# Four grouped weight tiles: high parts feature by feature, low parts last and on VectorE

## The chip, the cores and the metric

One core of one Trainium2 chip runs the whole program. The metric is device time in microseconds for one execution, the median of several runs of the same program.

## What is computed

The program takes 512 tokens of width 1024 through a gMLP layer and a FoX attention layer, each followed by a SwiGLU feed-forward network (FFN), and then through a block of mLSTM and indexer-selected attention with a gated embedding at its end. All inputs, weights and results are float32. What matters here are three products of a normalised and modulated activation with a weight matrix:

```python
def swiglu(h, w_gu, w_down):          # FFN 0 and FFN 1: w_gu is 1024 x 5632
    gu = h @ w_gu
    g, u = jnp.split(gu, 2, axis=-1)
    return (jax.nn.silu(g) * u) @ w_down
...
    u = rmsnorm(h, norm_in[i])        # second block
    proj = u @ w_in[i]                # its first columns here: the indexer's
```

## The kernel before

**Three passes per product.** Every large product is exact to more than one float32r pass: each operand is split into a high part `hi` (rounded to float32r) and a low part `lo` (the rest), and `mm3` (line 415) sums three passes of TensorE, weights' high by activations' high (line 416), high by low (line 417), and weights' low by activations' high (line 418). In a feature-major product the weights are the stationary operand.

**Preparing a weight tile.** `wsplit` (line 274) loads 128x1024 weights to a buffer `raw` (four buffers, loads issued on SP's queue, line 271), copies them to `whi` on ScalarE (line 279) and subtracts to get `wlo` (line 282). `share` decides which engine subtracts: with `share=n` every n-th low part, counted by a program-wide counter `lo_n`, goes to GpSimd, the others to VectorE. There are four buffers each of `whi` and `wlo`.

**Feature-major products.** `gemm_a` (line 420) gives out^T, a tile of 128 outputs by 512 tokens at a time, with 8 feature tiles k of 128 to sum over. Its first `group` tiles are taken together and by halves of the tokens, since the second 256 tokens of the activation come later:

```python
for c in halves:
    for (wh, wl), pt in zip(ws, accs):
        for k in range(KD):
            mm3(pt[0:m, c], wh[...k...], wl[...k...], hi[k][:, c], lo[k][:, c], ...)
```

So a group of four tiles is 2 halves x 4 tiles x 8 features x 3 passes = 192 passes of 256 columns, tile by tile. Three calls have a group: the FFN's at line 586 (twice, with `GG = (1, 1)`) and the indexer's at line 1226 (`IG = 1`). With these constants all four low parts of each group are made on GpSimd.

**What comes before a group.** In all three places the preceding product is a token-major `gemm_b` (line 443) whose last chunks go token tile by token tile (128 tokens each). As a token tile is through, `post` (line 534) evacuates its PSUM accumulator `acc` (a square on ScalarE, line 541, and a multiply on VectorE, line 542), adds it to the residual (line 552) and normalises the row (`norm_rows`, lines 366, 367, 359, 360, 370). After each second token tile, `to_T` (line 372) transposes two tiles on TensorE (line 384), scales them on ScalarE (line 407, or 405 in the second block) and splits them on VectorE: `hi` by a cast (line 408) and `lo` by a subtraction (line 409). So half the tokens of the group's activation come while `gemm_b` still works on the other half.

**PSUM.** The pool `ps` has four accumulators `acc` and four banks `tp`. The four token tiles of `gemm_b` hold the four accumulators; a group of four weight tiles takes the same four, each after its evacuation.

**Order.** Every engine works through its own instructions in a fixed order. Apart from one section of layer 0, that order is not the written one: the compiler places an instruction that is ready by its own estimate ahead of earlier-written ones that are not, and prefers the earlier-written where several are ready.

Of the kernel before, what the change touches and what calls it, by code (L numbers as in the profile page):

```python
"""One-core Trainium2 kernel: a gMLP layer, a FoX attention layer (each with a SwiGLU FFN), then an
mLSTM + indexer-sparse-attention block with a per-layer-embedding gate, for 512 tokens of width 1024.

Large products run as three float32r passes over exactly split operands (hi*hi + hi*lo + lo*hi).
"""
# [55 lines left out]
# ------------------------------------------------------------------ host layout  # L61
def _wa(w):
    """[K, N] -> [N/128, 128 (k in tile), K/128 * 128]: stationary chunks of 128 outputs."""
    k, n = w.shape
    return np.ascontiguousarray(
        w.reshape(k // P, P, n // P, P).transpose(2, 1, 0, 3).reshape(n // P, P, (k // P) * P))


def _wb(w):
    """[K, N] -> [N/512, K/256, 128, 2 * 512]: moving chunks of two k tiles by 512 outputs."""  # L70
    k, n = w.shape
    return np.ascontiguousarray(
        w.reshape(k // 256, 2, P, n // 512, 512).transpose(3, 0, 2, 1, 4).reshape(n // 512, k // 256, P, 1024))
# [26 lines left out]
def layout(i):  # L100
# [33 lines left out]
    # gMLP  # L134
# [14 lines left out]
    # FoX  # L149
# [8 lines left out]
    # second block  # L158
# [3 lines left out]
    # rows of the last tile: keys 0-63, input gates 64-67, forget gates 96-99, indexer weights 100-107  # L162
# [28 lines left out]
# ------------------------------------------------------------------ kernel body  # L191
def body(tc, nc, a):
    V, S_, G, PE = nc.vector, nc.scalar, nc.gpsimd, nc.tensor

    with ExitStack() as es:
# [55 lines left out]
        # ---------------- constants  # L251
# [14 lines left out]
        # ---------------- weights: load, split  # L266
# [7 lines left out]
        def wsplit(src, n=1024, share=0, alloc=None, raw=None):  # L274
            """share: every share-th low part on GpSimd"""
# [9 lines left out]
        # ---------------- modulation vectors, worked off between weight chunks  # L285
# [21 lines left out]
        def fill(n=1):  # L307
            """one column's load, and the product for the one loaded before"""
# [25 lines left out]
        def gain(csc, gname):  # L334
            """gain * (1 + scale), a column per feature tile"""
# [5 lines left out]
        def gb_row(cg, gname):  # L341
            """gate * gain, on every partition"""
# [13 lines left out]
        # ---------------- norms, transposes  # L356
        def rsq(out, ss, scale):
            """out = 1 / sqrt(ss * scale + eps)"""
# [3 lines left out]
        def norm_rows(xr, out):  # L362
            """out = xr / rms(xr), a token tile in two halves"""
# [8 lines left out]
        def to_T(ts, xn, g, sh, hi, lo, js=range(KD), spill=None):  # L372
            """token-major halves of the tiles ts -> feature-major hi, lo; what is transposed goes
            to spill as well"""
# [39 lines left out]
        # ---------------- products  # L414
# [5 lines left out]
        def gemm_a(h, w, n, evac, m=P, group=0, nfill=0, share=0, gshare=1):  # L420
            """out^T tile i (m outputs by 512 tokens), weights stationary. The first group goes by
            halves of the tokens, since the second half of h comes later."""
            hi, lo = h
            i = 0
            while i < n:
                run = list(range(i, min(n, i + (group if i == 0 and group else 1))))
                halves = (slice(0, 256), slice(256, 512)) if i == 0 and group else (slice(0, 512),)
                ws, accs = [], []
                for q in run:
                    ws.append(wsplit(w[q], KD * m, gshare if len(run) > 1 else share))  # L430
                    accs.append(acc())
                    if len(run) == 1:
                        fill(nfill if i >= 10 or not group else 0)
                for c in halves:
                    for (wh, wl), pt in zip(ws, accs):
                        for k in range(KD):
                            mm3(pt[0:m, c], wh[:, k * m:(k + 1) * m], wl[:, k * m:(k + 1) * m],
                                hi[k][:, c], lo[k][:, c], k == 0, k == KD - 1)
# [4 lines left out]
        def gemm_b(h, w, groups, kt, evac, head=False, tail=0, nfill=0, share=0, raws=(), hshare=1):  # L443
            """out tile (g, t): 128 tokens by 512 outputs, activations stationary. The last chunks
            of a group (all of them in the first with head) go token tile by token tile."""
# [25 lines left out]
        def chunks_a(h, w, n, evac):  # L471
            """gemm_a's weight chunks for between(): source, number of steps, step"""
# [15 lines left out]
        def chunks_b(h, w, g, kt, evac):  # L488
            """gemm_b's weight chunks of a group for between()"""
# [17 lines left out]
        def between(chunks, share=1):  # L507
            """products to be placed between the steps of something else: a function that emits the
            next n steps (all that are left without n)"""
# [24 lines left out]
        def post(gb, xsrc, xdst, alloc, done):  # L534
            """x += gate * rms_norm(y), then x / rms(x) by token tiles"""
# [23 lines left out]
        def halves(h, g, sh, spill=None):  # L559
            """takes normalised token tiles; transposes two at a time"""  # L560
# [33 lines left out]
        # ================= layer 0: gMLP  # L594
# [5 lines left out]
        with tc.tile_pool(name="l0", bufs=20) as p0:  # L600
# [8 lines left out]
            # loads in the order of their use: per-layer embedding, x, modulation with weights  # L609
# [16 lines left out]
            # relative bias by distance 511 - m  # L626
# [26 lines left out]
            def norm2(t):  # L653
                """two token tiles"""
# [14 lines left out]
            with tc.manual_schedule(engines={mybir.EngineType.Activation, mybir.EngineType.DVE, mybir.EngineType.PE, mybir.EngineType.SP}):  # L669
                S_.activation(crow, crow, AF.Silu)  # L670
                # brings in the table of the square root
# [31 lines left out]
                # the first products start as the modulation of each feature tile is there  # L703
# [50 lines left out]
                # both gains and the scale of the attention's scores, for the keys  # L754
# [40 lines left out]
            def ready(g):  # L795
                """the spatial weights of a group of features, and its values normalised"""
# [46 lines left out]
        # ================= FFN 0  # L843
# [10 lines left out]
        # ================= layer 1: FoX attention  # L854
# [762 lines left out]
```

## Time and profile before

| | before |
|---|---|
| runs | 1936.7 to 1945.61 us, median 1938.3 us (3 runs) |
| profiled execution, span | 1936.7 us |
| profiled execution, own time beside the span | 1936.7 us, the lowest of the runs: nothing to add to the span |
| mean granted clock of TensorE | 0.982 |
| TensorE (PE) busy | 1880.1 us, 97% |
| VectorE (DVE) busy | 1123.1 us, 58% |
| ScalarE (ACT) busy | 794.6 us, 41% |
| GpSimd (POOL) busy | 375.8 us, 19% |

PE is TensorE's matmul stream, PEld its weight loads, DVE VectorE, ACT ScalarE, POOL GpSimd, SP the queue that issues the DMAs. In a timeline each line has start, duration, engine, source line, operation, output <- input, count, and in brackets the idle time just before with what ended it. In a table of stretches each line has the stretch, its length, busy time of each engine with the number of instructions begun in brackets, the granted TensorE clock (1.00 is 2.4 GHz, 0.50 is 1.2 GHz), the DMA engines' busy share and GB/s.

### The profile page before, as it was taken

The page shows a single profiled execution, that of the slowest core. Times are in us where ns is not written, and L with a number is a line of the kernel's source. Part 1 is how long each engine was busy: PE and PEld are TensorE (multiplying, and loading weights), DVE is VectorE, ACT ScalarE, POOL GpSimd, SP SyncE. Part 2 cuts the span into 40 slices and gives each one's busy share as a digit, 9 for nine tenths or more (in the row PEclk, how much of TensorE's full clock was granted, in tenths as well). Part 3 has the DMA queues.
Part 4 walks back from the last instruction along what each step waited for, and adds up shares of the span by engine and source line. Part 5 has one row for each costly group of instructions (what it writes and reads, how often), then busy time and mean ns, then how long its engine had stood idle before and what let it go on. Part 6 is the DMA issues. An engine that isn't in the chain of part 4 may idle for free.

```text
span 1936.7 us, 23791 instructions
## 1 busy us (share of the span) xinstructions
PE 1880.1 (97%) x8688; PEld 1523.1 (79%) x8688; DVE 1123.1 (58%) x2132; ACT 794.6 (41%) x1395; POOL 375.8 (19%) x216
## 2 busy tenths in 40 slices
PE   7999998999999999999998999999989999999998
PEld 5788877888878877877777888888876877888887
DVE  7879735677762275367757333322365967856534
ACT  5334324422231255477655222222344246455334
POOL 2100123222220013433322111100020353022011
PEclk9999999999999999999998999999987999999999
DMA  8674753477763446733512322233243633322522
GB/s 330 235 274 137 251 194 109 147 265 260 260 219 109 141 138 205 247 120 126 172 67 97 112 94 96 98 109 126 103 136 98 187 129 111 115 93 88 191 96 100
DMA packets 106191, 299.46 MB, mean 155 GB/s; under 512 B 11893, under 2 KB 14749, under 8 KB 106074
## 3 DMA queue, kind: packets, MB, share of 16 engines
q1 hardware_dynamic: 106074, 297.94, 45.3%
q8 instruction: 69, 1.13, 0.2%
q14 instruction: 48, 0.39, 0.1%
HBM read 266.35 MB, written 34.16 MB: 155 GB/s over the span
## 4 chain that ended last, share of the span: by engine, by line
PE 78%; DVE 11%; DMA 7%; issue 2%; ACT 2%; POOL 0%; SPq 0%; DVEq 0%; ACTq 0%
PE acc L416 22%; PE acc L418 22%; PE acc L417 22%; DMA raw<-in_ada 6%; DVE raw L302 3%; PE tp L975 2%; PE tp L1016 2%; DVE d L302 1%; PE tp L1001 1%; PE tp L974 1%; DVE h L408 1%; PE tp L384 1%; DVE wlo L282 1%; DVE h L409 1%; PE tp L815 1%
## 5 line engine op out<-in xcount | busy, mean ns | idle before, releaser
L279 ACT ACTIVATE whi<-raw 128x1024 fp32r<-128x1024 f32 x293 | 309.9, 1059 | 679.4 <-PE acc L418 305.5
L282 POOL TENSOR_TENSOR wlo<-raw,whi 128x1024 fp32r<-128x1024 f32 x124 | 305.1, 2464 | 1368.3 <-ACT whi L279 1189.1
L417 PE MATMUL acc<-h,whi 128*128 128x512 f32 (+1 forms) x1112 | 418.2, 376 | 10.5 <-DVE h L409 10.4
L416 PE MATMUL acc<-h,whi 128*128 128x512 f32 (+1 forms) x1112 | 418.6, 376 | 5.5 <-DVE h L408 5.2
L418 PE MATMUL acc<-h,wlo 128*128 128x512 f32 (+1 forms) x1112 | 417.5, 375 | 3.3 <-DVE wlo L282 2.7
L282 DVE TENSOR_TENSOR wlo<-raw,whi 128x1024 fp32r<-128x1024 f32 x169 | 212.4, 1259 | 312.6 <-ACT whi L279 312.2
L417 PEld LDWEIGHTS acc<-h,whi 128*128 128x128 f32 x1112 | 212.5, 191 | 48.6 <-DVE h L409 12.7
L416 PE MATMUL acc<-whi,h 128*128 128x512 f32 x608 | 242.5, 399 | 7.9 <-DVE h L408 6.5
L416 PEld LDWEIGHTS acc<-h,whi 128*128 128x128 f32 x1112 | 212.8, 191 | 43.2 <-DVE h L408 6.0
L418 PEld LDWEIGHTS acc<-h,wlo 128*128 128x128 f32 x1112 | 212.7, 191 | 41.9 <-DVE wlo L282 4.5
L417 PE MATMUL acc<-wlo,h 128*128 128x512 f32 x608 | 240.0, 395 | 3.2 <-DVE wlo L282 3.2
L418 PE MATMUL acc<-whi,h 128*128 128x512 f32 x608 | 240.8, 397 | 0.0
L302 DVE SCALAR_TENSOR_TENSOR raw<-raw,cact 128x1024 f32<-128x1024 f32 x96 | 148.9, 1562 | 75.4 <-DMA raw<-in_ada 69.8
L416 PE MATMUL acc<-whi,s 128*128 128x512 f32 (+1 forms) x488 | 190.4, 390 | 0.7 <-DVE t L1308 0.7
L417 PE MATMUL acc<-wlo,s 128*128 128x512 f32 (+1 forms) x488 | 190.7, 391 | 0.0
L418 PE MATMUL acc<-whi,s 128*128 128x512 f32 (+1 forms) x488 | 190.2, 390 | 0.0
L416 PEld LDWEIGHTS acc<-whi,h 128*128 128x128 f32 x608 | 115.5, 190 | 34.2 <-DVE h L408 7.6
L417 PEld LDWEIGHTS acc<-wlo,h 128*128 128x128 f32 x608 | 115.2, 189 | 27.0 <-DVE wlo L282 4.1
L418 PEld LDWEIGHTS acc<-whi,h 128*128 128x128 f32 x608 | 115.2, 189 | 26.5 <-DVE h L409 2.4
L416 PEld LDWEIGHTS acc<-whi,s 128*128 128x128 f32 x488 | 91.7, 188 | 20.1 <-DVE t L1308 1.1
L417 PEld LDWEIGHTS acc<-wlo,s 128*128 128x128 f32 x488 | 91.7, 188 | 18.8
L418 PEld LDWEIGHTS acc<-whi,s 128*128 128x128 f32 x488 | 91.7, 188 | 18.6
(349 smaller groups left out, 2416.4 us busy)
## 6 DMA issues: line engine op xcount, KB each, us to landing
raw<-in_ada SPq DMA_DIRECT2D x96, 512.0 KB, 4.3
raw<-in_w_gu SPq DMA_DIRECT2D x88, 512.0 KB, 3.5
raw<-in_w_dn SPq DMA_DIRECT2D x44, 512.0 KB, 3.2
scr<-t SPq DMA_DIRECT2D x60, 256.0 KB, 4.1
raw<-in_w_o SPq DMA_DIRECT2D x20, 512.0 KB, 3.4
row<-scr SPq DMA_DIRECT2D x36, 256.0 KB, 3.4
d<-in_ada SPq DMA_DIRECT2D x16, 512.0 KB, 6.9
raw<-in_w_v SPq DMA_DIRECT2D x16, 512.0 KB, 5.2
```

The lines of the kernel that those rows point to most:

```text
L279: S_.activation(hi[:, 0:n], raw[:, 0:n], AF.Copy)
L282: e.tensor_sub(lo[:, 0:n], raw[:, 0:n], hi[:, 0:n].bitcast(F32))
L302: V.scalar_tensor_tensor(raw, raw, 1.0, cact[0], ALU.mult, ALU.mult, accum_out=modc[:, col:col + 1])
L384: PE.transpose(src[:, i * P:(i + 1) * P], xn[t][j // 4][:, (j % 4) * P:(j % 4 + 1) * P], ident[:])
L408: V.tensor_copy(hi[j][:, c], fj)
L409: V.tensor_sub(lo[j][:, c], fj, hi[j][:, c].bitcast(F32))
L416: PE.matmul(out, lh, rh, start=start, stop=False)
L417: PE.matmul(out, lh, rl, start=False, stop=False)
L418: PE.matmul(out, ll, rh, start=False, stop=stop)
L815: PE.matmul(sp[:, n * P:(n + 1) * P], vt[n, i // 4][:, o], rows[i // 4][:, o], start=True, stop=True)
L975: PE.matmul(sp[:, o:o + w], qs_[me, qs], kl[me, 0:w], start=False, stop=True)
L1016: PE.matmul(po[:, s * P:512], vd[s, hd // 4][:, hq * P:(hq + 1) * P], pt[:, PTO[s]:PTO[s] + n], start=(q == 0 and s == 0), stop=(q == 1 an ...
```

## The change

In a group, the weights of all four tiles are loaded and their high parts copied first. For each half of the tokens, the passes that need only the high parts then go feature by feature over all four tiles, and the passes with the low parts come after them, tile by tile. The low parts are written after the first half's high passes, and always on VectorE; `gshare` is no longer read and the counter `lo_n` no longer counts them. Tiles outside a group are unchanged. A group still has 192 passes of 256 columns, 4 loads, 4 copies and 4 subtractions. The rest of the diff removes comments and docstrings.

```diff
             while i < n:
                 run = list(range(i, min(n, i + (group if i == 0 and group else 1))))
-                halves = (slice(0, 256), slice(256, 512)) if i == 0 and group else (slice(0, 512),)
                 ws, accs = [], []
-                for q in run:
-                    ws.append(wsplit(w[q], KD * m, gshare if len(run) > 1 else share))
+                if len(run) == 1:
+                    ws.append(wsplit(w[i], KD * m, share))
                     accs.append(acc())
-                    if len(run) == 1:
-                        fill(nfill if i >= 10 or not group else 0)
-                for c in halves:
-                    for (wh, wl), pt in zip(ws, accs):
+                    fill(nfill if i >= 10 or not group else 0)
+                    for k in range(KD):
+                        mm3(accs[0][0:m], ws[0][0][:, k * m:(k + 1) * m], ws[0][1][:, k * m:(k + 1) * m],
+                            hi[k], lo[k], k == 0, k == KD - 1)
+                else:
+                    raws = []
+                    for q in run:
+                        accs.append(acc())
+                        raws.append(load_w(w[q], KD * m))
+                        ws.append([tile_of(pw, q_, F32R, 1024) for q_ in ("whi", "wlo")])
+                        S_.activation(ws[-1][0], raws[-1], AF.Copy)
+
+                    for nh, c in enumerate((slice(0, 256), slice(256, 512))):
                         for k in range(KD):
-                            mm3(pt[0:m, c], wh[:, k * m:(k + 1) * m], wl[:, k * m:(k + 1) * m],
-                                hi[k][:, c], lo[k][:, c], k == 0, k == KD - 1)
+                            for (wh, _), pt in zip(ws, accs):
+                                PE.matmul(pt[:, c], wh[:, k * P:(k + 1) * P], hi[k][:, c], start=nh == k == 0, stop=False)
+                                PE.matmul(pt[:, c], wh[:, k * P:(k + 1) * P], lo[k][:, c], start=False, stop=False)
+                        for (wh, wl), pt, raw in zip(ws, accs, raws):
+                            if nh == 0:
+                                V.tensor_sub(wl, raw, wh.bitcast(F32))
+                            for k in range(KD):
+                                PE.matmul(pt[:, c], wl[:, k * P:(k + 1) * P], hi[k][:, c], start=False,
+                                          stop=nh == 1 and k == KD - 1)
                 for q, pt in zip(run, accs):
                     evac(q, pt)
```

## Rows read from the trace of the kernel before

**Rows 1.** The page's busy times: us (share of the span) and instructions.

```profile
PE 1880.1 (97%) x8688; PEld 1523.1 (79%) x8688; DVE 1123.1 (58%) x2132; ACT 794.6 (41%) x1395; POOL 375.8 (19%) x216
```

**Rows 2.** Table of stretches: the three groups, and an undisturbed piece of the second.

```profile
324.50:357.60 33.10, 28.07 (x209) 26.32 (x209) 24.90 (x42) 16.08 (x30) 10.75 (x5) 0.95 0.35 122
1030.40:1065.60 35.20, 29.21 (x210) 27.75 (x209) 25.30 (x43) 15.97 (x30) 10.43 (x5) 0.85 0.31 114
1405.40:1440.90 35.50, 29.16 (x210) 27.39 (x209) 24.02 (x45) 15.31 (x31) 10.26 (x6) 0.86 0.39 135
...
1054.00:1064.00 10.00, 10.00 (x86) 10.00 (x85) 5.09 (x6) 5.53 (x7) 2.40 (x1) 1.00 0.15 54
```

**Rows 3.** The same table: the stretches of low granted clock within the groups.

```profile
332.00:335.40 3.40, 3.24 (x15) 2.74 (x13) 2.97 (x6) 1.91 (x6) 2.28 (x1) 0.55 0.82 296
1035.50:1045.50 10.00, 6.46 (x26) 5.85 (x27) 8.75 (x14) 3.76 (x11) 4.99 (x2) 0.50 0.65 240
1410.90:1420.80 9.90, 5.83 (x24) 4.96 (x24) 8.07 (x12) 3.50 (x10) 4.29 (x2) 0.50 0.60 208
```

**Rows 4.** Timeline of TensorE, first group: gemm_b's last pass, the group's first, two waits.

```profile
324.34 0.39 PE L418 MATMUL acc<-whi,s 128*128 128x512 f32 x1
324.56 0.28 PE L416 MATMUL acc<-h,whi 128*128 128x256 f32 x1
...
328.32 0.39 PE L417 MATMUL acc<-h,whi 128*128 128x256 f32 x1 [1.49 <-DVE h L409]
...
330.68 0.38 PE L416 MATMUL acc<-h,whi 128*128 128x256 f32 x1 [1.85 <-DVE h L408]
```

**Rows 5.** Timeline of VectorE, first group; the last line ends the second half's features.

```profile
322.86 2.89 DVE L552 SCALAR_TENSOR_TENSOR s<-t,sm,s 128x512 f32<-128x512 f32 x1
325.68 2.59 DVE L409 TENSOR_TENSOR h<-t,h 128x256 fp32r<-128x256 f32 x1
328.19 2.43 DVE L408 CAST h<-t 128x256 fp32r<-128x256 f32 x1
330.54 0.74 DVE L552 SCALAR_TENSOR_TENSOR s<-t,sm,s 128x512 f32<-128x512 f32 x1
331.21 0.41 DVE L409 TENSOR_TENSOR h<-t,h 128x256 fp32r<-128x256 f32 x1
331.54 0.28 DVE L408 CAST h<-t 128x256 fp32r<-128x256 f32 x1
...
336.09 0.68 DVE L542 TENSOR_TENSOR t<-acc,gb 128x512 f32<-128x512 f32 x1
...
346.37 0.43 DVE L409 TENSOR_TENSOR h<-t,h 128x256 fp32r<-128x256 f32 x1
```

**Rows 6.** Timeline of GpSimd, first group.

```profile
322.73 7.74 POOL L282 TENSOR_TENSOR wlo<-raw,whi 128x1024 fp32r<-128x1024 f32 x3 [18.53 <-ACT whi L279]
333.12 2.37 POOL L282 TENSOR_TENSOR wlo<-raw,whi 128x1024 fp32r<-128x1024 f32 x1 [2.65 <-ACT whi L279]
```

**Rows 7.** Timeline of ScalarE, first group.

```profile
322.96 1.09 ACT L279 ACTIVATE whi<-raw 128x1024 fp32r<-128x1024 f32 x1
325.85 0.63 ACT L366 ACTIVATE junk<-s 128x512 bf16<-128x512 f32 x1 [1.79 <-DVE s L552]
...
326.48 1.04 ACT L279 ACTIVATE whi<-raw 128x1024 fp32r<-128x1024 f32 x1
...
333.25 0.58 ACT L541 ACTIVATE junk<-acc 128x512 bf16<-128x512 f32 x1
...
350.18 1.28 ACT L579 ACT_TABLE_LOAD   x1
351.47 0.60 ACT L579 ACTIVATE t<-acc 128x512 f32<-128x512 f32 x1
```

**Rows 8.** The page's costliest groups: low parts made on VectorE, whole span (busy us, mean ns).

```profile
L282 DVE TENSOR_TENSOR wlo<-raw,whi 128x1024 fp32r<-128x1024 f32 x169 | 212.4, 1259 | 312.6 <-ACT whi L279 312.2
```

**Rows 9.** Timeline of TensorE where the keys' product begins (w_k, line 1082).

```profile
711.83 0.50 PE L417 MATMUL acc<-wlo,h 128*128 128x512 f32 x1 [1.94 <-DVE wlo L282]
```

## The prediction

> **What bounds the kernel.** I read the page's busy times first: TensorE is busy for 1880.1 of 1936.7 us [rows 1], so what the change can win is what TensorE loses in the three groups. The table of stretches comes next, with each group from its first pass to its last [rows 2]. Length less TensorE's busy time is idle: 33.10 - 28.07 = 5.0 us in the first (FFN 0), 35.20 - 29.21 = 6.0 in the second (FFN 1), 35.50 - 29.16 = 6.3 in the third (indexer). The granted clock is 0.95, 0.85 and 0.86 over them. Nearly all of that is 0.50, the 1.2 GHz level, in one stretch of each [rows 3]. In an undisturbed piece 86 passes of 256 columns begin in 10 us, 0.116 us each [rows 2]; the slow stretches hold 15, 26 and 24 passes that at this pace take 1.7, 3.0 and 2.8 us, and TensorE was busy with them for 3.2, 6.5 and 5.8 us. So the low clock cost 1.5 + 3.4 + 3.0 = 7.9 us. With the idle 17.3 that is **25.2 us** above undisturbed groups, which would be 33.1 - 5.0 - 1.5 = 26.6, 25.8 and 26.2 us long. This checks: 192 x 0.116 = 22.3 us, and the transposes of the second token pair are in there too.
>
> What TensorE waits for is in its timeline of the first group [rows 4]: a low part of the activation (line 409) for 1.49 us, a high part (line 408) for 1.85. The timeline of VectorE [rows 5] says why these are late: a cast of 0.28 us took 2.43, a subtraction of 0.41 took 2.59, a residual add of 0.74 took 2.89. They stand exactly under GpSimd's low parts, 322.73 to 330.47 and again from 333.12 [rows 6]; as soon as GpSimd pauses at 330.5, the same operations have their short times again. So the three VectorE operations lost 2.15 + 2.2 + 2.15 = 6.5 us to GpSimd, and TensorE, at 0.35 us per feature in tile-by-tile order, had no other work that was ready.
>
> **The change part by part.**
>
> *Low parts leave GpSimd.* Four subtractions a group, some 10 us of GpSimd [rows 6], go away, and with them the stretched operations. From 322.86 on VectorE's six operations in rows 5 need 0.7 + 0.4 + 0.3 + 0.7 + 0.4 + 0.3 = 2.8 us instead of 9, and the rest of the last two features 0.4 + 0.3 + 0.4 more: all eight are there at 326.8.
>
> *Feature by feature.* One feature now feeds 4 tiles x 2 passes = 8 x 0.116 = 0.93 us, where VectorE needs 0.41 + 0.28 = 0.7 us to make one [rows 5]. So once started, TensorE doesn't overtake VectorE. The last feature is wanted 6.5 us after the start at 324.56 [rows 4], at 331, 4 us after it is there. The activation's waits, 17.3 us of idle less a few tenths, go.
>
> *Low parts on VectorE.* 4 x 1.26 = 5.0 us a group [rows 8]. They are wanted from the end of the 64 high passes, 7.4 us after the start, one every 8 x 0.116 = 0.93 us. VectorE has from 326.8 until then, with the rest of the third token tile's work and the fourth tile's start beside it, and lost 6.5 us less before. I cost the first half at nothing. If the cover fails, the second half pays: its features come from the fourth token tile's chain (square, multiply, two adds, two squares, two scalings, transposes). Even if all 5.0 us lie ahead of that chain, it has the 6.5 us back that GpSimd took. Zero, up to 1.2 us a group.
>
> *All four tiles at the start.* This is the new wait. The third and fourth copies of weights stand on ScalarE behind the squares of line 366, which waited for the stretched residual add [rows 7]. Without the stretch I chain from 324.05: twice (0.63 + 1.04) gives the fourth copy at 327.4. Later still is the fourth accumulator: it is the one that gemm_b's last token tile used until 324.34 + 0.39 [rows 4], and is free after line 541 (0.58 and its read-out, some 0.8) and line 542 (0.68) [rows 5, 7]: about 327.4 + 0.3 + 0.8 + 0.7 = 329.2, 4.6 us after the start. Three tiles offer 48 passes, 5.6 us, meanwhile. The engines' order is not the written one: on ScalarE the group's copies (line 279), written after all of gemm_b's evacuation, run ahead of line 541 of the last token tile [rows 7]. So I expect the fourth tile's passes to be placed late, and a wait of only what the placing is off. Bounds: nothing, and 4.6 less the 0.7 us of the first feature on three tiles, 3.9. The nearest row is a wait of 1.94 us for a low part on VectorE at the keys' product [rows 9]; between it and nothing I take **1.0 us a group, 3 us in all**.
>
> *After the group.* High weights' buffers of all four tiles now come free only some 4.4 us before the group's end (32 low passes, 3.7 us, and up to 6 high ones), low ones from 24 passes, 2.8 us, before it on. The next tile needs a copy (1.04) and a subtraction (1.26, on GpSimd 2.4), done 1.6 or 0.3 us before the end. Its accumulator needs the first tile's evacuation, a table load of 1.28 and 0.60 [rows 7] after the first tile's last pass, 0.9 us before the end. All fits, barely; between nothing and 1.9 us I take 0.3 a group, 1 us.
>
> *Queues.* The next tiles' loads on SP wait for the low parts to free `raw`, with stores of line 553 queued behind them. Low parts end on VectorE around the time at which they did on GpSimd, and the next copy finds no buffer before the second half is nearly through: nothing. GpSimd's queue loses 12 instructions and nobody waits behind them. `lo_n` counts 4 fewer per group, so where `share` is 3 (keys' product, FFN 1, tail of w_o) other low parts fall to GpSimd: 1.26 against 2.4 us, either way, so 0 with 2 us to each side.
>
> **Sum:** 25.2 - 3 - 1 = 21.2 us. In the profiled execution's time 1936.7 - 21.2 = 1915.5; the median is 1.6 above that execution, so **1917 us**. Bounds of this case: all won and 2 us more (1911) to 1.2 us lost in each second half, 1.9 at each end, 1.9 at each start and 2 elsewhere: 25.2 - 3 x 5 - 2 = 8, so 1930.
>
> **A rule against it.** Rows 2 and 3 show a tile-by-tile order whose clock fell to the 1.2 GHz level in every group, after waits [rows 4]. The Trainium skill, TensorE: Matmul & The Clock Gate, section on HAM oscillation, advises to take all contraction tiles of one output tile before anything that waits, so that the array stays warm; it speaks for the old order. The trace disagrees here: that order was the one that went cold.
>
> **Rivals.**
>
> *The clock falls all the same (the rule above is its page).* Small waits at the start, 1 us a group as above, and the low clock stays as dear as in the second and third group, 3.2 us [rows 3]. For: in the second group the fall came 5 us after the first pass [rows 2, 3]. Against: waits get shorter and single. 25.2 - 3 - 1 - 9.6 = 11.6 us: 1927.
>
> *The fourth accumulator decides.* If TensorE's order is the written one, feature 0 waits 3.9 us a group for line 542, and the clock falls, 3.2 us as above: 7.1 x 3 = 21.3 us paid of 25.2. Against: the order seen on ScalarE [rows 7]. 1938.3 - 4 = 1934, no change by the bound below.
>
> *Slower: low parts at the end of VectorE's queue.* They are written after everything the second half's features need. If they also run after it, TensorE stands in front of the first half's low passes from 336 (7.4 us and transposes after the start) until the last feature (340.3: the end of the last line of [rows 5], 346.8, less 6.5) and one subtraction, 341.5: 5.5 us; then 3 x (1.26 - 0.93) = 1.0; then the clock, 3.2 us and as much again since TensorE would be fully busy in it, say 4.5. 11 us a group, 33 against 25.2: 1946. It turns slower from the point where the first low part is ready over 8.4 - 1.0 - 4.5 = 2.9 us behind the high passes' end (8.4 is a third of 25.2). Against: 5 us of work that is ready early finds VectorE's short waits for ScalarE on the way.
>
> *It does nothing:* if the stretches were not GpSimd's. Rows 5 and 6 leave little room; less than 1 in 50, within "same".
>
> **Chances.** Measurements tell 0.5%, 9.7 us, from no change. Forecast 0.68, clock 0.10: both faster, 0.78. Fourth accumulator 0.12 and little else 0.03: same, 0.15. Low parts late, 0.05, is by its price at the edge; with the less likely rest, slower 0.07. The range takes the forecast with its bounds and the clock's case: 1911 to 1931.
>
> **What would show it.** In the changed profile: no operation of lines 408, 409 or 552 above 0.8 us within the groups; no GpSimd work there; TensorE idle under 1.5 us and granted clock 1.00 in each group, 27 to 28 us long; a short wait near the fourth tile's first pass, ended by line 542 or 279. It is wrong if TensorE waits 3 us or more for line 542, or for line 282's successor on VectorE at the end of the first half, or if the clock still falls without such waits.

## The result and the profile after

The changed kernel takes 1920.93 us, the median of 4 runs (1914.79 to 1922.82), beside 1939.11 us for the kernel before (4 runs, 1936.70 to 1945.61). The ratio is 0.9889, with an interval of 0.9864 to 0.9915: faster by over 0.5%. The forecast was 1917 with a range of 1911 to 1931. The profiled execution has a span of 1919.2 us and an own time of 1920.94, 17.5 us less span than before. (In every run of the experiments the time is 1.7 to 1.9 us above the span. So the execution that was profiled before, with a span of 1936.7, is more likely the run of 1938.3 than, as the table says, that of 1936.7. The forecast is the same from either: 1938.3 - 21.2 = 1917.) Behind the edit the line numbers are 15 higher: 542 is now 557, 552 is 567, 916 is 931. The new passes stand at lines 446, 447 and 452, the new low parts at 450, the new copies at 441.

The page's busy times after, which answer to [rows 1]:

```profile
PE 1870.9 (97%) x8688; PEld 1516.6 (79%) x8688; DVE 1113.8 (58%) x2144; ACT 793.0 (41%) x1395; POOL 350.1 (18%) x204
```

TensorE and VectorE have as many passes and operations to do as before (VectorE 12 more), and both are busy for less time. GpSimd has lost 12 instructions and 26 us.

The table of stretches after: the three groups, and the 15 us behind the third. Columns: stretch, length, busy time of PE, PEld, DVE, ACT and POOL with the instructions that begin in it, granted clock, DMA share, GB/s.

```profile
328.40:354.03 25.63, 25.59 (x210) 25.07 (x209) 16.91 (x41) 13.85 (x29) 1.78 (x1) 1.00 0.42 127
1028.34:1053.90 25.56, 25.51 (x209) 24.88 (x208) 16.86 (x40) 13.68 (x29) 2.41 (x1) 1.00 0.39 124
1393.70:1419.30 25.60, 25.56 (x209) 24.87 (x208) 17.35 (x41) 12.48 (x27) 1.73 (x1) 1.00 0.48 151
1419.26:1434.26 15.00, 11.16 (x44) 8.76 (x44) 10.41 (x12) 7.78 (x13) 1.15 (x2) 0.89 0.43 147
```

Against [rows 2] the groups are 25.6 us long in place of 33.1, 35.2 and 35.5. TensorE is busy through all of each, and the granted clock is 1.00, the 2.4 GHz level, from end to end. With the borders of the two tables the span splits like this:

| stretch | before | after | difference | forecast |
|---|---|---|---|---|
| start to first group | 324.50 | 328.40 | +3.9 | 0 |
| the three groups | 103.80 | 76.79 | -27.0 | -22.2 |
| first to second group | 672.80 | 674.31 | +1.5 | 0, 2 either way |
| second to third group | 339.80 | 339.80 | 0.0 | |
| third group to end | 495.80 | 499.90 | +4.1 | +1.0 (all three groups) |
| sum | | | -17.5 | -21.2 |

So the groups gave more than was forecast, and some of it was lost in two places outside them. The timeline of VectorE in the first group shows why the groups are short; the last line ends the second half's features, as in [rows 5]:

```profile
327.93 0.74 DVE L567 SCALAR_TENSOR_TENSOR s<-t,sm,s 128x512 f32<-128x512 f32 x1
328.59 0.42 DVE L409 TENSOR_TENSOR h<-t,h 128x256 fp32r<-128x256 f32 x1
328.92 0.28 DVE L408 CAST h<-t 128x256 fp32r<-128x256 f32 x1
329.13 1.22 DVE L450 TENSOR_TENSOR wlo<-raw,whi 128x1024 fp32r<-128x1024 f32 x1
...
332.41 0.67 DVE L557 TENSOR_TENSOR t<-acc,gb 128x512 f32<-128x512 f32 x1
...
335.07 1.21 DVE L450 TENSOR_TENSOR wlo<-raw,whi 128x1024 fp32r<-128x1024 f32 x1
...
345.16 0.42 DVE L409 TENSOR_TENSOR h<-t,h 128x256 fp32r<-128x256 f32 x1
```

The residual add takes 0.74 us where it took 2.89, the subtraction 0.42 for 2.59, the cast 0.28 for 2.43. The four low parts lie between them at 1.22 each, the last one through at 336.3, 7.9 us after the group's first pass.

The two losses outside the groups stand in the list of what TensorE waited for (us in total, times, longest), here the first and fourth line of the whole span:

```profile
PE acc L416 <- DVE t L557: 6.9, 1, 6.9
...
PE acc L416 <- DVE s L931: 3.8, 1, 3.8
```

The first is in layer 0's product with `w_ao` (line 855), which the change doesn't touch, some 47 us before the first group. Before the change the same wait (for line 542 there) was half as long:

```profile
PE acc L416 <- DVE t L542: 3.2, 1, 3.2
```

The second is the first pass behind the third group; TensorE's timeline has it with what follows:

```profile
1423.05 0.47 PE L416 MATMUL acc<-h,whi 128*128 128x512 f32 x1 [3.78 <-DVE s L931]
1423.35 0.39 PE L417 MATMUL acc<-h,whi 128*128 128x512 f32 x1
...
1424.84 0.63 PE L416 MATMUL acc<-h,whi 128*128 128x512 f32 x1
1425.26 0.63 PE L417 MATMUL acc<-h,whi 128*128 128x512 f32 x1
```

Passes of 512 columns begin 0.23 us apart at first and 0.43 us apart from about 1424.2 to 1427.4: behind the wait the clock falls to the 1.2 GHz level, 0.52 in the table from 1424.0 to 1427.4. That is some 8 passes x 0.2 = 1.6 us, with the wait 5.4 us in that place. Before the change nothing was lost there (TensorE is busy for 14.94 of the 15 us from 1441.0 on). From the third group to the end the span is 4.1 us longer.

The timelines of VectorE and GpSimd there:

```profile
1418.45 3.72 DVE L282 TENSOR_TENSOR wlo<-raw,whi 128x1024 fp32r<-128x1024 f32 x2
1422.21 1.41 DVE L931 TENSOR_TENSOR s<-acc,s 64x512 fp32r<-64x512 f32 x2
```

```profile
1417.57 2.39 POOL L282 TENSOR_TENSOR wlo<-raw,whi 128x1024 fp32r<-128x1024 f32 x1 [164.16 <-PE acc L452]
```

In VectorE's queue two low parts of the next product's weights stand before the second half of the first evacuation (`stack`, line 931), and they take 3.72 us together in place of 2.4, since the first of them falls under a low part on GpSimd.

### The profile page after: what moved, and what is told of

It reads as the page before. It is cut to its first block, busy times and chain, and to the rows that moved or that the text cites. A ratio compares the mean times of both kernels' runs of the same rounds, so it can differ in the third digit from the quotient of the medians.

```text
span 1919.2 us, 23780 instructions
## 1 busy us (share of the span) xinstructions
PE 1870.9 (97%) x8688; PEld 1516.6 (79%) x8688; DVE 1113.8 (58%) x2144; ACT 793.0 (41%) x1395; POOL 350.1 (18%) x204
## 4 chain that ended last, share of the span: by engine, by line
PE 76%; DVE 11%; DMA 8%; issue 2%; ACT 2%; POOL 0%; SPq 0%; DVEq 0%; ACTq 0%
PE acc L416 21%; PE acc L418 21%; PE acc L417 21%; DMA raw<-in_ada 7%; DVE raw L302 4%; PE tp L990 2%; PE tp L1031 1%; DVE d L302 1%; PE tp L1016 1%; DVE wlo L282 1%; PE tp L989 1%; PE acc L452 1%; PE acc L447 1%; PE acc L446 1%; PE tp L384 1%
## 5 line engine op out<-in xcount | busy, mean ns | idle before, releaser
L279 ACT ACTIVATE whi<-raw 128x1024 fp32r<-128x1024 f32 x281 | 296.7, 1058 | 668.2 <-PE acc L418 298.0
L282 POOL TENSOR_TENSOR wlo<-raw,whi 128x1024 fp32r<-128x1024 f32 x112 | 279.2, 2495 | 1376.0 <-ACT whi L279 949.0
L282 DVE TENSOR_TENSOR wlo<-raw,whi 128x1024 fp32r<-128x1024 f32 x169 | 217.0, 1286 | 315.0 <-ACT whi L279 296.3
L416 PE MATMUL acc<-h,whi 128*128 128x512 f32 x920 | 362.0, 393 | 4.1 <-DVE s L931 3.8
L418 PE MATMUL acc<-h,wlo 128*128 128x512 f32 x920 | 360.9, 392 | 4.0 <-DVE wlo L282 4.0
L417 PE MATMUL acc<-h,whi 128*128 128x512 f32 x920 | 360.2, 392 | 0.0
L418 PEld LDWEIGHTS acc<-h,wlo 128*128 128x128 f32 x920 | 173.8, 189 | 42.5 <-DVE wlo L282 5.9
L416 PEld LDWEIGHTS acc<-h,whi 128*128 128x128 f32 x920 | 174.1, 189 | 41.7 <-issue 5.8
L417 PEld LDWEIGHTS acc<-h,whi 128*128 128x128 f32 x920 | 173.9, 189 | 35.8
```

Of the source, the lines that this page charges most:

```text
L279: S_.activation(hi[:, 0:n], raw[:, 0:n], AF.Copy)
L282: e.tensor_sub(lo[:, 0:n], raw[:, 0:n], hi[:, 0:n].bitcast(F32))
L416: PE.matmul(out, lh, rh, start=start, stop=False)
L417: PE.matmul(out, lh, rl, start=False, stop=False)
L418: PE.matmul(out, ll, rh, start=False, stop=stop)
```

## The experiments

Theory A, the one of the prediction: GpSimd's low parts stretch VectorE's operations, the activations come late, TensorE idles and loses its clock; moving the low parts to VectorE is what gains. Rival B: the new order of the passes is what gains, by giving TensorE other work while a feature is late. Theory C, for the loss behind the third group: the new order ends four tiles within the last 3.7 us, and their evacuations come in one bunch. The first four kernels ran on one chip, with the kernel before at 1945.41 us (13 runs). The runs of one kernel differ by 5 to 14 us there, so medians a few us apart don't tell kernels apart, and the stretches of the profiles are compared beside them.

**1. The old order, low parts on VectorE.** The kernel before with two constants changed:

```diff
-GG = (1, 1)
+GG = (0, 0)
-IG = 1
+IG = 0
```

> The kernel before with one constant changed: the four low parts of each group go to VectorE, in the old tile-by-tile order. Theory A (the stretching of VectorE by GpSimd was the cause): no VectorE operation of the groups above 1.3 us, groups of 27 to 29 us instead of 33 to 35.5, with a wait of 1 to 2 us per group for the first low parts, which this order wants at once; in all 12 to 20 us faster than before. Theory B (the order is the cause: tile by tile, TensorE uses up a feature in 0.35 us and VectorE makes one in 0.7): groups of 31 us or more, less than 8 us won, with waits for lines 408 and 409.

Measured: 1914.56 us (1912.18 to 1918.09), ratio 0.9855 (0.9818 to 0.9893). The third group in the table of stretches (the first two are 26.55 and 26.68 us long at clock 1.00), and TensorE's waits of the first:

```profile
1394.44:1420.65 26.21, 25.61 (x209) 24.97 (x208) 19.51 (x44) 13.95 (x29) 2.87 (x2) 1.00 0.55 174
```

```profile
PE acc L416 <- ACT whi L279: 0.5, 1, 0.5
PE acc L418 <- DVE wlo L282: 0.4, 1, 0.4
```

Two constants win about as much as the whole change, and the groups give 24.4 of the 27.0 us that they give there. They are still 0.6 to 1.1 us longer than in the changed kernel, by short waits for a copy of weights and for a low part.

**2. The new order, low parts on GpSimd.** The changed kernel with one letter changed at line 450:

```diff
-                                V.tensor_sub(wl, raw, wh.bitcast(F32))
+                                G.tensor_sub(wl, raw, wh.bitcast(F32))
```

> The changed kernel with its low parts on GpSimd again: the new order alone. Theory A: the VectorE operations are stretched to 2.4 to 2.9 us again, features come late, and TensorE waits 2 us or more in each group, which are 28 to 32 us long. Theory B: the order gives TensorE enough other work to ride over the stretches; groups of 25.6 to 26.5 us, as in the changed kernel, and the same time as it within 0.3%.

Measured: 1947.1 us (1941.06 to 1951.62), ratio 1.0017 (0.9997 to 1.0038). Stretches of the groups, then VectorE's timeline in the first, with GpSimd at work there from 324.00 to 331.76:

```profile
325.80:361.07 35.27, 28.28 (x209) 27.49 (x208) 20.89 (x40) 14.38 (x29) 9.91 (x5) 0.90 0.28 93
1036.63:1071.43 34.80, 28.35 (x209) 27.61 (x208) 21.41 (x40) 14.27 (x29) 10.42 (x5) 0.90 0.27 91
1411.29:1447.41 36.12, 30.10 (x209) 29.35 (x207) 21.65 (x42) 13.58 (x28) 8.96 (x5) 0.81 0.34 112
```

```profile
326.94 2.58 DVE L409 TENSOR_TENSOR h<-t,h 128x256 fp32r<-128x256 f32 x1
329.44 2.48 DVE L408 CAST h<-t 128x256 fp32r<-128x256 f32 x1
...
332.50 0.41 DVE L409 TENSOR_TENSOR h<-t,h 128x256 fp32r<-128x256 f32 x1
```

The order alone gives nothing: the stretched operations, the idle time and the low clock are all back. Rival B falls. The waits are others than before the change (in the second group 3.9 us for a copy of high weights, line 441, and 2.6 for a transpose's input): the new order doesn't wait for features one by one, but the delay of VectorE still comes out in full.

**3. High passes tile by tile, low parts last.** The changed kernel with the two loops of the high passes exchanged:

```diff
-                        for k in range(KD):
-                            for (wh, _), pt in zip(ws, accs):
+                        for (wh, _), pt in zip(ws, accs):
+                            for k in range(KD):
```

> The changed kernel, with the passes of the high parts tile by tile instead of feature by feature; low parts last and on VectorE as in the change. If taking the features over all four tiles matters by itself, the first tile (0.23 us per feature) runs into VectorE (0.7 us per feature and other work between) and TensorE waits 1.5 to 3 us in each group, with groups of 27 to 29 us. If putting the low parts last and on VectorE is all that matters, TensorE waits under 0.5 us and the groups stay at 25.6 to 26 us.

Measured: 1917.82 us (1914.07 to 1919.57), ratio 0.9868 (0.9831 to 0.9905). The first group:

```profile
328.75:354.35 25.60, 25.57 (x209) 25.02 (x208) 17.03 (x41) 15.87 (x30) 1.61 (x1) 1.00 0.42 126
```

The other two are 25.74 and 25.51 us long, and TensorE waits for nothing in any. So feature by feature isn't needed; what the new order adds to experiment 1 is that low parts come last, and that is worth its short waits, 0.6 to 1.0 us a group. Behind the third group the wait for line 931 is 2.6 us.

**4. Second half tile by tile.** The first half as in the change; in the second half each tile has its three passes at once, so that the four tiles end 3 us apart:

```diff
-                    for nh, c in enumerate((slice(0, 256), slice(256, 512))):
+                    c = slice(0, 256)
...
+                    c = slice(256, 512)
+                    for (wh, wl), pt in zip(ws, accs):
+                        for k in range(KD):
+                            mm3(pt[:, c], wh[:, k * P:(k + 1) * P], wl[:, k * P:(k + 1) * P], hi[k][:, c], lo[k][:, c],
+                                False, k == KD - 1)
```

> The changed kernel with the second 256 tokens of each group tile by tile with all three passes, as before the change, so that the tiles are through one after the other and their evacuations spread over the second half. Theory C (the 3.8 us wait behind the indexer's group comes of four evacuations standing together at the group's end): that wait and the 1.4 us of low clock behind it go. What it may cost: the second half's first tile takes a feature in 0.35 us where VectorE makes one in 0.7, so up to 1.5 us of waits inside each group. Net against the changed kernel: 0 to 5 us faster. If the wait has another cause (GpSimd stretching the next tiles' low parts on VectorE), it stays at 2.5 us or more.

Measured: 1913.75 us (1910.71 to 1916.71), ratio 0.9846 (0.9801 to 0.9891). The groups are 25.51, 25.65 and 25.49 us long, so the second half waits for nothing. The 15 us behind the third group, against the fourth line of the table of the changed kernel:

```profile
1418.08:1433.08 15.00, 14.94 (x69) 12.10 (x68) 8.93 (x12) 11.98 (x16) 0.00 (x0) 1.00 0.40 125
```

69 passes begin there in place of 44, the clock stays at 1.00, and from the group's end to the end of the span it is 495.9 us in place of 499.9. What theory C expected came out. But the edit does more than spread the evacuations: it also spreads the next weights' low parts. VectorE's begin at 1410.66 and 1416.40, before and after GpSimd's (1413.62 to 1416.02), and take 1.22 us each, so the stretch is gone too. Experiment 6 takes the two apart.

The next four kernels ran together on one chip, with the kernel before at 1944.87 us (9 runs), and ask what the two losses outside the groups are made of.

**5. Layer 0's `w_ao`, low parts on VectorE.** The changed kernel with line 856 changed:

```diff
-                   nfill=0.75, share=2)
+                   nfill=0.75, share=0)
```

> The changed kernel, and in layer 0's product with w_ao the low parts that went to GpSimd (every second weight tile) go to VectorE too. In the profile of the changed kernel TensorE waits 6.9 us there for VectorE's L557 (3.2 us before the change), because VectorE's L302 or L282 beside each GpSimd low part takes 2.4 to 3.4 us in place of 1.2, which frees a buffer late and sends the next weight loads beside the next ada load. Theory S (that stretch is the cause): no L302, L282 or L557 over 1.5 us between 240 and 285 us, the wait of TensorE at L557 falls to 3.5 us or less, the first group starts at 325.0 us or earlier in place of 328.4, and the time is 3 to 6 us below that of the changed kernel run again beside it. Rival D (the loads of ada and w_ao come late whatever the engine): the wait stays at 6 to 7 us, the start at 328 us, the time within 1 us.

Measured: 1912.08 us (1909.24 to 1917.14), ratio 0.9838 (0.9814 to 0.9861), 5.6 us below the changed kernel beside it (experiment 8), with runs that overlap. First the changed kernel's VectorE and GpSimd in that product, then VectorE in the experiment:

```profile
243.71 2.41 DVE L302 SCALAR_TENSOR_TENSOR raw<-raw,cact 128x1024 f32<-128x1024 f32 x1 [3.62 <-DMA s<-in_x]
...
276.95 3.35 DVE L282 TENSOR_TENSOR wlo<-raw,whi 128x1024 fp32r<-128x1024 f32 x1
280.22 2.47 DVE L557 TENSOR_TENSOR t<-acc,gb 128x512 f32<-128x512 f32 x4
```

```profile
242.65 2.39 POOL L282 TENSOR_TENSOR wlo<-raw,whi 128x1024 fp32r<-128x1024 f32 x1 [6.44 <-ACT whi L279]
...
275.87 3.35 POOL L282 TENSOR_TENSOR wlo<-raw,whi 128x1024 fp32r<-128x1024 f32 x1 [9.07 <-ACT whi L279]
```

```profile
241.90 1.23 DVE L302 SCALAR_TENSOR_TENSOR raw<-raw,cact 128x1024 f32<-128x1024 f32 x1 [2.20 <-DMA raw<-in_ada]
...
274.55 1.22 DVE L282 TENSOR_TENSOR wlo<-raw,whi 128x1024 fp32r<-128x1024 f32 x1
275.69 2.48 DVE L557 TENSOR_TENSOR t<-acc,gb 128x512 f32<-128x512 f32 x4
```

The evacuation of line 557 begins at 275.7 in place of 280.2, the first group starts at 322.5, and TensorE's wait is 1.8 us in place of 6.9:

```profile
PE acc L416 <- DVE t L557: 1.8, 1, 1.8
```

So it is the same collision at another place, and it isn't the loads that are late by themselves. (Between the first and the second group this profile is some 7 us shorter than that of experiment 8, where nothing was edited; only the part before 322.5 is put down to the edit.)

**6. First two `w_aqk` tiles, low parts on VectorE.** The changed kernel with line 1292 changed:

```diff
-            gemm_a(h, a["w_aqk"], 2, ev_a, share=2)
+            gemm_a(h, a["w_aqk"], 2, ev_a, share=0)
```

> The changed kernel, with both low parts of the first two w_aqk weight tiles on VectorE (one of the two was on GpSimd, 1417.57 us, 2.39 us long, and stretched a VectorE L282 to about 2.5 us). It tells apart why TensorE waits 3.8 us for VectorE's L931 after the third group. Theory S (the stretch by GpSimd is the larger part): the wait falls to 2.6 us or less, the clock stays 1.00, and the time falls by 1.3 to 3 us against the changed kernel beside it. Theory Q (four tiles end together and VectorE has the next weights' low parts queued ahead of their evacuations, wherever these are made): the wait stays at 3 to 5 us and the low clock behind it stays; time within 1 us.

Measured: 1916.54 us (1914.93 to 1923.78), ratio 0.9865 (0.9841 to 0.9889). TensorE behind the third group, then VectorE ahead of it:

```profile
1419.40 0.53 PE L416 MATMUL acc<-h,whi 128*128 128x512 f32 x1 [2.42 <-DVE s L931]
1419.74 0.63 PE L417 MATMUL acc<-h,whi 128*128 128x512 f32 x1
```

```profile
1416.17 2.36 DVE L282 TENSOR_TENSOR wlo<-raw,whi 128x1024 fp32r<-128x1024 f32 x2
1418.56 1.41 DVE L931 TENSOR_TENSOR s<-acc,s 64x512 fp32r<-64x512 f32 x2
```

Both theories have a part. Of the 3.8 us, 1.4 was the stretch (the two low parts take 2.36 us in place of 3.72); 2.4 remain, which are the evacuation queued behind the next weights' low parts, and the clock falls all the same (0.66 from 1419.4 to 1424.4). Whether the time gains can't be told: 1.1 us between medians whose runs differ by 9.

**7. Experiments 4 and 5 together.**

```diff
-                   nfill=0.75, share=2)
+                   nfill=0.75, share=0)
...
+                    c = slice(256, 512)
```

> The version of the fourth experiment (second half of the columns tile by tile) with w_ao's low parts on VectorE in layer 0, as in the fifth. If both effects are real and add: groups of 25.5 us, no wait after the third group, first group at 325 us or earlier, and 6 to 10 us below the changed kernel beside it, so about 1911. If layer 0's wait comes from the loads: 3 to 6 us below the changed kernel.

Measured: 1908.12 us (1905.80 to 1910.76), ratio 0.9814 (0.9794 to 0.9835), 9.6 us below experiment 8. Groups of 25.48, 25.65 and 25.50 us from 324.8 on, a wait of 2.1 us in layer 0, none behind the third group: in the profile the two add up.

**8. The changed kernel again**, with no edit.

> The changed kernel once more, on the chip of the three others, as what they are measured against: 1915 to 1923 us, groups of 25.4 to 25.7 us, the wait after the third group 3 to 4 us. Whether the first group starts near 324.6 or near 328.4 us tells whether the late start is tied to the change (it was 328.4 to 328.8 in four profiles with the groups' low parts on VectorE) or falls out differently from execution to execution.

Measured: 1917.68 us (1912.98 to 1923.44), ratio 0.9867 (0.9844 to 0.9889). The wait in layer 0 is 6.2 us, the first group starts at 328.66, the wait behind the third group is 3.8 us. So the late start is there again. It is in all six profiles in which the groups' low parts are on VectorE and those of `w_ao` half on GpSimd (328.4 to 329.2), and in neither of the two with the groups' low parts on GpSimd (324.5, 325.8), although the instructions up to there are the same. In the kernel before, line 302 ran from 241.56, 0.7 us ahead of GpSimd's low part at 242.26, and kept its 1.23 us; in the changed one a load came later and it fell under the low part. What makes that load late was not found, and six against two may be chance. What the lateness costs is plainer. In all six, one of VectorE's last two operations ahead of line 557 (line 302 or line 282) began under GpSimd's last low part of that product and took 2.8 to 3.4 us. In the other two both had begun before it, and each took 1.2. Not all of a start is the collision's: the version of experiments 7 and 10, with none of it in `w_ao`, starts its first group at 324.75 in one and at 322.11 in the other.

The last four carry the theory to the whole kernel; two ran beside each other with the kernel before at 1942.41 us (9 runs), two more with it at 1941.49 us (9 runs).

**9. Every low part on VectorE.** Experiment 7 with one line of `wsplit` (line 281) changed:

```diff
-            e = G if share and lo_n[0] % share == 0 else V
+            e = V
```

> The seventh experiment's version with every low part of the kernel on VectorE: the 104 that GpSimd still makes (257 us of GpSimd's time) become 104 of VectorE's 1.25 us, so VectorE's busy time goes from 1110 to about 1240 us less what is no longer stretched. Theory S, carried to the whole kernel (a low part costs less on VectorE than the stretch it causes from GpSimd): 2 to 8 us below the version it is made from, TensorE's waits for GpSimd's low parts (1.1 us) gone, those for VectorE no larger in sum. Rival B (in the stages where VectorE is busiest, 80 to 90% of a slice between 100 and 250 us, its queue is what TensorE waits for): new waits of TensorE for VectorE there, 5 us or more, and a time above that version's.

**10. Experiment 7 again**, beside it.

> The seventh experiment's version once more, beside the one with all low parts on VectorE: 1905 to 1911 us, groups of 25.5 us, no wait after the third group.

Measured: 1893.16 us (1893.02 to 1894.69) for 9, ratio 0.9745 (0.9724 to 0.9766); 1907.55 us (1907.11 to 1910.93) for 10, ratio 0.9821 (0.9799 to 0.9843). The page's busy times, and its line for line 302 (products of the weights `ada` with a vector; busy us, mean ns), first of 10, then of 9:

```profile
PE 1871.1 (98%) x8688; PEld 1516.7 (80%) x8688; DVE 1111.7 (58%) x2152; ACT 793.5 (42%) x1395; POOL 325.9 (17%) x196
...
L302 DVE SCALAR_TENSOR_TENSOR raw<-raw,cact 128x1024 f32<-128x1024 f32 x96 | 145.0, 1520 | 73.3 <-DMA raw<-in_ada 71.2 <-issue 1.5
```

```profile
PE 1865.7 (99%) x8688; PEld 1514.5 (80%) x8688; DVE 1153.5 (61%) x2256; ACT 793.5 (42%) x1395; POOL 76.1 (4%) x92
...
L302 DVE SCALAR_TENSOR_TENSOR raw<-raw,cact 128x1024 f32<-128x1024 f32 x96 | 117.2, 1223 | 83.6 <-DMA raw<-in_ada 83.1
```

14.4 us more, where 2 to 8 were expected. VectorE took over 104 operations of 1.25 us, 130 us, and is busy for only 42 us longer; the other 88 us are what its operations no longer spend beside GpSimd, in line 302 alone 0.3 us on each of 96. TensorE's waits sum to 19.3 us in place of 28.8, and it is busy for 5.4 us less. Rival B of that expectation, VectorE as the bound, falls.

**11. The kernel before, every low part on VectorE**: the same line, and nothing else.

> The kernel before, its order of passes kept, with every low part of the kernel on VectorE: one line of it. If the stretch of VectorE by GpSimd is all that the groups lose, it comes to the time of the ninth experiment (1893.2 us) and some 3 us more, since the old order waited 1 us per group for low parts on VectorE in the first experiment: 1894 to 1899 us, groups of 26.2 to 26.8 us. If the order of the passes is worth more than that once nothing is stretched: 1900 us or above.

**12. The changed kernel, every low part on VectorE.**

> The changed kernel with every low part on VectorE. Groups of 25.4 to 25.7 us as before; after the third group the wait of 2.4 us that the sixth experiment left with the low clock behind it, so 2 to 5 us above the ninth experiment (1893.2 us), which evacuates its tiles spread out: 1895 to 1899 us. Against the kernel before with all low parts on VectorE, beside it: 3 us faster by the groups, 2 to 4 us slower by the third group's end, so within 2 us. If that wait were free, 1893 to 1894 us.

Measured: 1896.63 us (1890.82 to 1898.80) for 11, ratio 0.9762 (0.9741 to 0.9783); 1893.88 us (1891.88 to 1902.29) for 12, ratio 0.9762 (0.9738 to 0.9786). The third group of 11, and TensorE behind the third group of 12:

```profile
1373.91:1400.12 26.21, 25.60 (x209) 24.96 (x208) 20.81 (x45) 13.94 (x29) 0.58 (x1) 1.00 0.58 184
```

```profile
1396.77 0.47 PE L416 MATMUL acc<-h,whi 128*128 128x512 f32 x1 [2.42 <-DVE s L931]
1397.08 0.39 PE L417 MATMUL acc<-h,whi 128*128 128x512 f32 x1
1397.31 0.40 PE L418 MATMUL acc<-h,wlo 128*128 128x512 f32 x1
```

One line in the kernel before is worth more than the change under study, and with that line in both, the old order and the new can't be told apart: the old pays 0.6 to 1.0 us a group, the new 2.4 us behind the third. Here the clock stays at 1.00 behind that wait, so 12 comes out better than was expected, level with 9 (which ran on another chip). In 11 TensorE's wait in layer 0's `w_ao`, with no low part on GpSimd, is as long as in the kernel before:

```profile
PE acc L416 <- DVE t L542: 3.1, 1, 3.1
```

## Why the prediction was right, point by point

**The cause holds.** That the 25.2 us were VectorE's stretched operations was shown twice over: experiment 1 takes GpSimd out and keeps the order, and the groups fall to 26.2 to 26.7 us at clock 1.00; experiment 2 keeps GpSimd in and takes the order, and they stay at 35. The undisturbed groups that the prediction worked out from the pace of a clean piece (26.6, 25.8, 26.2) were 1.8 us too long in sum, against the 76.8 us measured. The page SBUF — State Buffer of the Trainium skill, section "SBUF: two separate sides", says that GpSimd and VectorE (in an operation with two inputs in SBUF, or in a mode that takes both pairs of ports) lock a shared pair of ports against each other: whichever starts first has it for the whole instruction. The trace agrees: operations of 0.28 to 0.74 us took 2.43 to 2.89 beside GpSimd operations of 2.4 to 2.6.

**Feature by feature: this step fell.** The prediction let the activation's waits go because one feature feeds 0.93 us of passes where VectorE makes one in 0.7. With the loops exchanged (experiment 3) the groups are as short. Once VectorE isn't stretched, the first half's last feature is there at 332.4, 4.0 us after the group's start, and in either written order the instructions are placed so that TensorE waits for none. The order's own gain is the low passes at the end: 1.0, 0.9 and 0.7 us a group in experiment 3 against experiment 1.

**Low parts on VectorE, costed at nothing:** right. The four lie in the gaps, and no pass of a group waits for one.

**The fourth accumulator, 1.0 us a group:** nothing, its lower bound. Line 557 was done at 333.1, 4.7 us after the group's start, later than the 4.6 at which the prediction put it from the start, and yet TensorE waits for nothing in the group: the fourth tile's first pass is placed as the 41st, 40 x 0.12 = 4.8 us in. The compiler's placing fitted, as the prediction half expected and then didn't trust; the wait of [rows 9] was no guide. With the 1.8 us above these 3 us are the 4.8 us that the groups gave beyond the forecast.

**After the group, 1.0 us for all three:** this term was mis-sized. Behind the two FFN groups TensorE waits for nothing, behind the indexer's it waited 3.8 us and lost some 1.6 more to the clock. The prediction priced one evacuation for all, the FFN's, a table load and an activation on ScalarE [rows 7]. The indexer's goes through `stack`, two copies and two subtractions of 0.7 us a tile, and the next product's low parts are ahead of it in VectorE's queue, one of them on GpSimd and stretching another. Even the bound of 1.9 us was too low. Experiments 4 and 6 show the two parts.

**Nothing elsewhere, 0 with 2 us to each side:** mis-sized too; layer 0 alone took 3.9 us. The prediction looked for GpSimd's stretch in the groups alone, though half of the low parts of `w_ao` are GpSimd's as well. The 3.2 us that the list of waits of before has there need no stretch: with every low part on VectorE the wait is 3.1 us in experiment 11 and 0.7 in 12. With the stretch it grew to 6.9, and its size turns on which VectorE operations start inside GpSimd's 2.4 us (experiments 5 and 8).

That the time came out only 4 us above the forecast is in part luck, the balance of terms that erred by 4.8 us one way and by 8.5 the other (3.1 behind the group, 3.9 in layer 0, 1.5 between the groups, whose cause is open).

**The signs it named.** In the groups no operation of lines 408, 409 or 567 took over 0.75 us, and TensorE's idle time and clock are as forecast. The groups are shorter than the 27 to 28 us named, and the short wait at the fourth tile's first pass stayed away. GpSimd's one low part in each group is the next tile's, begun in the last 2.6 us.

**The rivals.** The clock didn't fall in any group. The prediction said that the trace speaks against the Trainium skill's advice (TensorE: Matmul & The Clock Gate, section on HAM oscillation) to take an output tile's contraction in one go, since the tile-by-tile order was the one that went cold. That reading was too quick: experiment 1 keeps that order at clock 1.00, and experiment 2 has the other order at 0.81 to 0.90. The waits decided, not the order. The page gives the advice for waits on a DMA; here the waits were for VectorE, so no run here tests it. The fourth accumulator and the low parts at the queue's end didn't come about.

## What to carry to other kernels

Before work is given to GpSimd because it is idle, look in VectorE's timeline at what runs beside it. Where short operations there take as long as GpSimd's one, the work can cost more on GpSimd than on a busy VectorE: here 104 operations, 130 us of work, moved to VectorE made it busy for only 42 us more and the kernel 14.4 us shorter. Find such a collision by comparing the shortest and the mean duration of one form over the whole span, not only in the stretch under study. And price an evacuation by the code of the group it belongs to, with what stands ahead of it in its engine's queue.

## What the runs showed that was not expected

Moving 130 us of work to an engine that was busy for 58% of the span cost it only 42: the other 88 us were paid back by operations that were no longer stretched. The Trainium skill's page Perfetto Trace Analysis, section "Optimizing Scalar/DVE Operations", says that work moved between VectorE and GpSimd might not help because of the shared port. The runs agree and go further: in this kernel the split cost 45 us (experiment 11 against the kernel before beside it, 1896.63 and 1941.49).

The same wait of 2.42 us behind the third group was followed by the 1.2 GHz level in experiment 6 (0.66 over the 5 us from 1419.4) and by 1.00 in experiment 12. TensorE was busy without a gap through the group ahead of it in both; what tells the two apart was not found.

In layer 0's `w_ao` product two neighbouring VectorE operations take turns at being stretched, and the start of line 302 against GpSimd's low part decides which. In the kernel before it ran from 241.56, 0.7 us ahead of GpSimd's at 242.26, and VectorE's low part behind it took 3.41 us (from 242.71). In experiment 8 it ran from 242.89, 0.7 us behind GpSimd's at 242.19, and took 2.77 itself. In the first case the next two loads, of `w_ao` and of `ada`, are issued 3.3 us apart (242.82 and 246.15), in the second 1.1 us apart (245.70 and 246.84).
